# Mixer A's lowest score level: products over the feature axis instead of window matmuls

## The chip, the cores and the metric

The kernel runs on one core of a Trainium2 chip. The metric is the device time of one execution in microseconds. Engines are called TensorE (PE in the profile, with its weight loads as PEld), VectorE (DVE), ScalarE (ACT), GpSimd (POOL) and SyncE (SP).

## The reference

A two-layer trunk over 512 tokens of width 2048, all in float32. Layer A is an HGRN2 mixer, layer B a forgetting attention; each has 16 heads of 128 features. The part that matters here is layer A's recurrence:

```
proj = rmsnorm(x) @ w_in          # q, fz, i, gate
log_f, k = from fz and a lower bound
S_t = diag(exp(log_f_t)) S_{t-1} + k_t v_t^T ;  o_t = S_t^T q_t
o = head_rmsnorm(o) * silu(gate);  x = x + o @ w_out
```

Unrolled, o_t is a sum over s <= t of score(t, s) v_s, with

```
score(t, s) = sum over features f of q_t[f] * k_s[f] * exp(b_t[f] - b_s[f])
b = cumulative sum of log_f
```

The decay depends on the feature, so scores are not a plain product of q and k.

## The kernel before

Tensors lie features by tokens, 128 x 512 for a head. Each float32 matmul is made of three: both sides are split in a high part in TensorE's float32r format and a low part (`split`, L439: ScalarE copies the high part, VectorE subtracts it), and high x high, low x high and high x low are summed in PSUM.

**Projections.** `group` (L220) multiplies 16 chunks (`kt`) of a weight block of 512 columns by the normalised input, 12 matmuls of 512 columns a chunk (L238-240 for values, L242-244 for the rest). Each chunk's weights arrive by DMA as `wr` and are split into `wh` and `wl`, three buffers each, one chunk ahead of use (`Chunks`, `w_split`). In layer A sixteen groups run in the order `q0 v0 q1 q2 v1 q3 g0 q4 v2 q5 q6 v3 q7 g1 g2 g3`; a `q` group gives q and the forget logits of two heads.

**Heads.** `mix_a(h)` (L606) is a generator: it emits one head's work in steps, each ending in `yield`. After each weight chunk `pump` runs two steps (`RATE_A = 2`), head after head; other places run steps when they need a head's buffers. Thus a head's work lies among the matmuls of later groups. The Tile framework orders the instructions of every engine by a simulated time line while building; each engine then runs its own queue in that order.

**Scores by levels.** A window is 128 tokens. Scores are computed in levels: pairs (t, s) within groups of 4 tokens (the lowest level), then groups of 16 and 64 (the loop over m = 4, 16), then halves of a window, then window against window. On each level q is first multiplied by decays for a distance d of 1, 2 or 3 (tile `e` and, on higher levels, `t1`, `tn`), so that a plain product with k gives scores. `win_scores` (L585) multiplies a window's k (`kh`, `kl`) by a row of q variants (`mh`, `ml`) into a PSUM bank, and `put_scores` (L575) copies, with a 0/1 mask (`masks`, `COPY_PREDICATED`, L583), those scores that belong to distance d into the score tile `at`, of 4 windows by 128 keys by 128 queries.

The lowest level (L624-657) takes q itself (d = 0, 128 columns a window) and three products `pr` (96, 64 and 32 columns a window): 320 columns for each of four windows, three matmuls each. A product for distance d is only wanted at queries t whose position in the group of 4 is at least d, and against one key, s = t - d; the matmul computes it against all 128 keys of the window, and the mask picks the wanted one. After the splits, q and k are multiplied in place by decays for the next level (L640, L645).

**A sum over features.** `sum_parts` (L328), used for norms, sums 128 partitions exactly: VectorE adds the lower half of the partitions to the upper (L333), VectorE makes the high part (L334) and the low part (L335) into the two halves of one tile, and a matmul with a 128 x 128 matrix of ones (L336) gives every output partition the total.

**After the scores**, `attend` multiplies them by the split values, `out_norm` norms the head, and the output projection follows once all heads are done. Layer B repeats the pattern with `mix_b`.

## Time and profile before

| what | value |
|---|---|
| time, median of 3 runs | 2014.63 us (2012.73 to 2015.29) |
| profiled execution, its time | 2013.94 us |
| span of that execution, first to last instruction | 2012.2 us |
| mean granted TensorE clock | 0.994 |
| busy share of the span: PE, DVE, ACT, POOL | 98%, 77%, 56%, 9% |
| matmuls | 10218 |
| chain that ended last: PE, DVE, DMA | 84%, 7%, 4% |

Rows of instruction groups give line, engine, operation, output and inputs, shapes and count, then total busy time and the mean time of one. In a time line the first column is the start, the second how long the merged instructions lasted from the first start to the last end. On one engine the next instruction can start before the last has ended, so the distance between starts can be shorter than the duration. Layer A's groups and heads take the span from about 50 to 850 us, its output projection goes to about 1050, layer B's groups to about 1850, its output projection to the end.

### The profile page before, as it was taken

To read this page: it belongs to the slowest core of one execution; us is meant where nothing else is said; L and a number is where in the kernel's file an instruction comes from. 1 tells how busy PE (TensorE), PEld (TensorE's weight loads), DVE (VectorE), ACT (ScalarE), POOL (GpSimd) and SP (SyncE) were. 2 spreads that over 40 slices of the span, in tenths; PEclk is the share of its full clock that TensorE was granted. 3 is DMA by queue.
4 is the path that set the end of the run, shared out by engine and by line. 5 is a ranking of instruction groups with operands and counts; after the bars stand their busy time and mean duration, and the time that the engine had idled before them with its cause. 6 is when DMAs were issued, how large, how long until landed. Compare 5 with 4: busy or idle time off the path is not lost.

```text
span 2012.2 us, 28874 instructions
## 1 busy us (share of the span) xinstructions
PE 1978.6 (98%) x10218; PEld 1696.5 (84%) x10218; DVE 1558.8 (77%) x3321; ACT 1130.1 (56%) x2311; POOL 172.8 (9%) x301
## 2 busy tenths in 40 slices
PE   9999999999999999989999999999999999999898
PEld 7888888888888888869987888888888888888898
DVE  7968987979798889698873677776766676688877
ACT  5646655657566466654443555655555556576332
POOL 3303110202122030000000000000000000000000
PEclk9999999999999999999999999999999999999999
DMA  5222222222222222244433222333233232223443
GB/s 189 74 87 82 74 84 75 83 79 79 84 74 74 74 84 84 84 142 140 149 118 95 94 87 87 95 89 95 84 89 93 92 95 89 90 84 111 132 156 105
DMA packets 61696, 195.01 MB, mean 97 GB/s; under 512 B 7904, under 2 KB 8032, under 8 KB 61552
## 3 DMA queue, kind: packets, MB, share of 16 engines
q1 hardware_dynamic: 61408, 193.17, 30.8%
q8 instruction: 80, 1.31, 0.3%
q14 instruction: 64, 0.52, 0.1%
q10 hardware_dynamic: 144, 0.01, 0.0%
HBM read 184.73 MB, written 8.42 MB: 96 GB/s over the span
## 4 chain that ended last, share of the span: by engine, by line
PE 84%; DVE 7%; DMA 4%; issue 2%; ACT 1%; POOL 1%; SPq 0%; DVEq 0%; ACTq 0%; POOLq 0%
PE gm L244 17%; PE gm L242 17%; PE gm L243 17%; PE gm L238 6%; PE gm L240 6%; PE gm L239 6%; DMA wr<-in_wb_q 2%; DVE w7l L441 2%; PE mx L590 2%; PE mx L589 2%; PE mx L588 1%; DMA wr<-in_wa_q 1%; PE mx L435 1%; PE mx L436 1%; PE mx L434 1%
## 5 line engine op out<-in xcount | busy, mean ns | idle before, releaser
L242 PE MATMUL gm<-xh,wh 128*128 128x512 f32 x1664 | 650.6, 392 | 0.1
L243 PE MATMUL gm<-xl,wh 128*128 128x512 f32 x1664 | 649.8, 391 | 0.0
L244 PE MATMUL gm<-xh,wl 128*128 128x512 f32 x1664 | 610.3, 392 | 1.1 <-DVE wl L441 1.1
L242 PEld LDWEIGHTS gm<-xh,wh 128*128 128x128 f32 x1664 | 313.1, 188 | 63.1 <-ACT wh L440 0.3
L243 PEld LDWEIGHTS gm<-xl,wh 128*128 128x128 f32 x1664 | 313.2, 188 | 62.7
L244 PEld LDWEIGHTS gm<-xh,wl 128*128 128x128 f32 x1664 | 311.3, 188 | 63.6 <-DVE wl L441 2.3
L440 ACT CAST wh<-wr 128x512 fp32r<-128x512 f32 x288 | 177.3, 620 | 155.7 <-PE gm L243 113.8
L441 DVE TENSOR_TENSOR wl<-wr,wh 128x512 fp32r<-128x512 f32 x288 | 204.7, 714 | 66.8 <-ACT wh L440 56.8
L147 ACT ACTIVATE wh<-wr,v_b_norm_w 128x256 fp32r<-128x256 f32 (+1 forms) x192 | 111.7, 584 | 186.4 <-PE gm L243 152.3
L148 DVE SCALAR_TENSOR_TENSOR wl<-wr,v_b_norm_w,wh 128x256 fp32r<-128x256 f32 (+1 forms) x192 | 109.3, 571 | 133.5 <-ACT wh L147 128.3
L239 PE MATMUL gm<-wl,xh 128*128 128x512 f32 x512 | 200.7, 392 | 0.0
L240 PE MATMUL gm<-wh,xl 128*128 128x512 f32 x512 | 200.2, 392 | 0.0
L238 PE MATMUL gm<-wh,xh 128*128 128x512 f32 x512 | 180.5, 392 | 1.5 <-DVE q L552 1.5
L147 ACT ACTIVATE wh<-wr,v_kv_norm_w 128x256 fp32r<-128x256 f32 (+1 forms) x192 | 110.1, 574 | 65.2 <-PE gm L240 48.3
L148 DVE SCALAR_TENSOR_TENSOR wl<-wr,v_kv_norm_w,wh 128x256 fp32r<-128x256 f32 (+1 forms) x192 | 109.3, 571 | 42.1 <-ACT wh L147 41.5
L583 DVE COPY_PREDICATED at<-masks,mx 128x128 f32<-128x128 uint8 (+4 forms) x448 | 108.8, 297 | 13.4 <-PE mx L590 13.0
L942 POOL TENSOR_SCALAR_AFFINE_SELECT s<-s 128x128 f32<-128x128 f32 x64 | 28.5, 445 | 1029.1 <-DVE s L941 1028.6
L238 PEld LDWEIGHTS gm<-wh,xh 128*128 128x128 f32 x512 | 95.9, 188 | 20.4 <-DVE q L552 1.8
L240 PEld LDWEIGHTS gm<-wh,xl 128*128 128x128 f32 x512 | 96.2, 188 | 19.0
L239 PEld LDWEIGHTS gm<-wl,xh 128*128 128x128 f32 x512 | 96.3, 188 | 18.8
L440 ACT CAST w7h<-wr 128x768 fp32r<-128x768 f32 x48 | 40.1, 835 | 100.7 <-PE mx L296 38.2
L440 ACT CAST kh<-k 128x512 fp32r<-128x512 f32 (+1 forms) x96 | 56.3, 587 | 44.1 <-PE mx L589 19.7
(225 smaller groups left out, 3852.6 us busy)
## 6 DMA issues: line engine op xcount, KB each, us to landing
wr<-in_wb_qk SPq DMA_DIRECT2D x64, 512.0 KB, 3.5
wr<-in_wa_qf SPq DMA_DIRECT2D x62, 512.0 KB, 3.5
wr<-in_wa_v SPq DMA_DIRECT2D x32, 512.0 KB, 3.5
wr<-in_wa_g SPq DMA_DIRECT2D x32, 512.0 KB, 3.5
wr<-in_wb_v SPq DMA_DIRECT2D x32, 512.0 KB, 3.5
wr<-in_wb_g SPq DMA_DIRECT2D x32, 512.0 KB, 3.5
wr<-in_wa_q SPq DMA_DIRECT2D x24, 512.0 KB, 3.5
wr<-in_wb_q SPq DMA_DIRECT2D x24, 512.0 KB, 3.6
```

Of the source, the lines that this page charges most:

```text
L147: S.activation(h[:, c], r[:, c], AF.Copy, scale=w[:, kt : kt + 1])
L148: V.scalar_tensor_tensor(l[:, c], r[:, c], w[:, kt : kt + 1], rd(h)[:, c], op0=ALU.mult, op1=ALU.subtract)
L238: PE.matmul(banks[j], xh, h, start=f, stop=False)
L239: PE.matmul(banks[j], xh, l, start=False, stop=False)
L240: PE.matmul(banks[j], xl, h, start=False, stop=e)
L242: PE.matmul(banks[j], h[:, c], Xh[kt], start=f, stop=False)
L243: PE.matmul(banks[j], h[:, c], Xl[kt], start=False, stop=False)
L244: PE.matmul(banks[j], l[:, c], Xh[kt], start=False, stop=e)
L440: S.copy(h, src)
L441: return V.tensor_sub(l, src, rd(h))
L583: V.copy_predicated(out, mv, data)
L589: PE.matmul(lv[:, base : base + n], kh[:, c], ml, start=False, stop=False)
```

## The change

In the lowest level the products are taken by elements. VectorE multiplies q by k (`p0`, 512 columns, distance 0), and the decayed, shifted q by k shifted back by d tokens (`pr`, 384, 256 and 128 columns for d = 1, 2, 3). `half_parts` adds the two partition halves of such a tile and puts the high part (ScalarE) and the low part (VectorE) into the two halves of another; a matmul with `ones` sums over the features. Its 128 output rows are all the same row of scores, and the masks of before pick, for each key, the columns of the queries at distance d, now for all four windows in one masked copy per distance. k is no longer split on this level. The tile `p0` takes a buffer of the tag `kl`; the two halves' tiles take one pair of `mh` and `ml`, where there were two pairs. The level takes two steps fewer of the generator.

```diff
+    def half_parts(x, hl):
+        half = P // 2
+        V.tensor_add(x[:half], x[:half], x[half:])
+        S.copy(hl[:half], x[:half])
+        V.tensor_sub(hl[half:], x[:half], rd(hl)[:half])
...
-        kh, kl = k_split(h, k)
-        pr = mt("pr", (P, NW, 192), 1)
-        for d, c0 in ((1, 0), (2, 96), (3, 160)):
+        p0 = rd(mt("kl", (P, T), 2, F32R))
+        pr = mt("pr", (P, 768), 1)
+        V.tensor_mul(p0, q, k)
+        for d, c0 in ((1, 0), (3, 384), (2, 512)):
             n = 4 - d
-            V.tensor_mul(
-                view(pr, c0, [[192, NW], [n, 32], [1, n]]),
-                view(q, d, [[P, NW], [4, 32], [1, n]]),
-                view(e, (d - 1) * T + d, [[P, NW], [4, 32], [1, n]]),
-            )
+            o = view(pr, c0, [[n, P], [1, n]])
+            V.tensor_mul(o, view(q, d, [[4, P], [1, n]]), view(e, (d - 1) * T + d, [[4, P], [1, n]]))
+            V.tensor_mul(o, o, view(k, 0, [[4, P], [1, n]]))
         yield
-        for w0 in (0, 2):
-            mh, ml = m_tiles(h)
-            for dst, src, step, n in ((0, q, P, P), (P, pr, 192, 192)):
-                d = [[320, 2], [1, n]]
-                split(view(src, w0 * step, [[step, 2], [1, n]]), view(mh, dst, d), view(ml, dst, d))
-            if w0:
-                (q and k times their decays, as below)
+        hl, hl0 = m_tiles(h)
+        half_parts(p0, hl0[:, :T])
+        half_parts(pr, hl)
+        V.tensor_mul(view(q, 0, [[4, P], [1, 4]]), view(q, 0, [[4, P], [1, 4]]), view(e, 0, [[4, P], [T + 1, 4]]))
+        kv = view(k, 0, [[4, P], [1, 3]])
+        V.tensor_mul(kv, kv, view(e, 2 * T + 3, [[4, P], [-T, 3]]))
+        yield
+        for x, w, parts in (
+            (hl0, T, ((0, 0),)),
+            (hl, T, ((1, 0), (3, 384))),
+            (hl[:, T:], 256, ((2, 0),)),
+        ):
+            lv = lv_bank()
+            PE.matmul(lv[:, :w], ones, x[:, :w], start=True, stop=True)
+            for d, c0 in parts:
+                put_scores(at, lv, 0, NW, c0, (4 - d) * 32, 1, d, d)
             yield
-            for i in range(2):
-                lv = lv_bank()
-                c = slice(i * 320, (i + 1) * 320)
-                win_scores(lv, 0, w0 + i, kh, kl, mh[:, c], ml[:, c], 320)
-                for d, c0 in ((0, 0), (1, P), (2, P + 96), (3, P + 160)):
-                    put_scores(at, lv, w0 + i, 1, c0, T, 1, d, d)
-                yield
```

## The prediction

> **What bounds the kernel now.** I read the first and fourth parts of the page, then the busy time of the engines by stretches. In the stretches the columns are the stretch, its length, the busy time of PE, PEld, DVE, ACT and POOL with instruction counts, the granted clock, the DMA share and GB/s.

> ```profile
> span 2012.2 us, 28874 instructions
> PE 1978.6 (98%) x10218; PEld 1696.5 (84%) x10218; DVE 1558.8 (77%) x3321; ACT 1130.1 (56%) x2311; POOL 172.8 (9%) x301
> ...
> PE 84%; DVE 7%; DMA 4%; issue 2%; ACT 1%; POOL 1%; SPq 0%; DVEq 0%; ACTq 0%; POOLq 0%
> ```
> ```profile
> 50.00:850.00 800.00, 797.42 (x3923) 676.30 (x3922) 685.35 (x1665) 493.40 (x1089) 126.94 (x204) 1.00 0.26 80
> ...
> 1850.00:2012.00 162.00, 145.69 (x1100) 139.95 (x1099) 126.27 (x211) 58.54 (x73) 0.00 (x0) 0.97 0.40 130
> ```

> TensorE sets the end: 84% of the chain. The change lies in mixer A, whose heads run beside the input projections from 50 to 850 us. There TensorE is busy for 797.4 of 800 us, so every matmul taken away is time, as long as nothing else takes over. VectorE is the candidate: 685 of 800 us, 86%, before anything is added. An average over 800 us hides what matters, so I cut out the stretches in which VectorE is densest:

> ```profile
> 70.00:100.00 30.00, 30.00 (x152) 25.48 (x151) 29.93 (x83) 17.22 (x44) 10.54 (x20) 1.00 0.24 71
> 170.00:210.00 40.00, 40.00 (x203) 34.18 (x202) 39.62 (x97) 23.86 (x58) 15.30 (x24) 1.00 0.26 78
> 230.00:250.00 20.00, 20.00 (x104) 17.06 (x103) 19.94 (x57) 12.93 (x35) 2.58 (x6) 1.00 0.24 79
> 350.00:390.00 40.00, 39.73 (x196) 33.37 (x196) 39.57 (x99) 26.97 (x63) 15.45 (x24) 1.00 0.25 80
> 450.00:500.00 50.00, 50.00 (x250) 42.68 (x249) 48.67 (x123) 36.53 (x91) 16.01 (x25) 1.00 0.27 84
> 550.00:590.00 40.00, 38.90 (x197) 32.92 (x196) 39.38 (x104) 25.97 (x62) 12.79 (x21) 1.00 0.24 78
> 600.00:630.00 30.00, 30.00 (x155) 25.66 (x154) 29.94 (x79) 20.12 (x48) 7.76 (x13) 1.00 0.21 70
> 730.00:770.00 40.00, 39.83 (x199) 33.72 (x198) 39.83 (x104) 24.16 (x59) 12.34 (x19) 1.00 0.25 73
> ```

> Adding up the rows: in 290 us VectorE is busy for 286.9, 98.9%, and TensorE for 288.5. Both engines are full at once. The same stretches for the multiply of q by its decay alone (L640, once a head, behind this level's products) count eleven of the sixteen heads; one of the eight rows and their sum:

> ```profile
> 170.00:210.00 40.00, 2.26 (x2) 1.00 0.26 78
> ...
> sum 290.00, DVE 12.08; mean DVE 1.51
> ```

> At 1.1 us each 12.08 us are eleven. So most of the levels that the change rewrites stand where VectorE has no time to give.

> **The change part by part.**

> TensorE. Per head twelve matmuls of 320 columns go (four windows, three products each) and three with the ones come, of 512, 512 and 256 columns. What a pipelined matmul costs is the distance between starts:

> ```profile
> 602.36 0.30 PE L588 MATMUL mx<-mh,kh 128*128 128x320 f32 x1
> 602.50 0.31 PE L589 MATMUL mx<-ml,kh 128*128 128x320 f32 x1
> 602.65 0.31 PE L590 MATMUL mx<-mh,kl 128*128 128x320 f32 x1
> 602.80 0.39 PE L240 MATMUL gm<-wh,xl 128*128 128x512 f32 x1
> 603.03 0.40 PE L238 MATMUL gm<-wh,xh 128*128 128x512 f32 x1
> ```

> Three of 320 columns take 0.44 us, 0.147 each; one of 512 takes 0.23. The 256 columns I price at the row above them, 0.147. Per head 12 x 0.147 - (0.23 + 0.23 + 0.147) = 1.15 us less, for 16 heads 18.4 us. If VectorE keeps up, that is the whole result.

> VectorE, removed and added. Here too the distance between starts counts, since short instructions overlap. A stretch of this very level (the first row merges eight copies of several widths):

> ```profile
> 184.49 1.55 DVE L583 COPY_PREDICATED at<-masks,mx 128x128 f32<-128x128 uint8 x8
> 185.91 0.55 DVE L441 TENSOR_TENSOR ml<-q,mh 128x384 fp32r<-128x384 f32 x1
> 186.38 0.45 DVE L583 COPY_PREDICATED at<-masks,mx 128x64 f32<-128x64 uint8 x2
> 186.60 0.60 DVE L441 TENSOR_TENSOR ml<-pr,mh 128x384 fp32r<-128x384 f32 x1
> 187.11 0.47 DVE L583 COPY_PREDICATED at<-masks,mx 128x96 f32<-128x96 uint8 x2
> 187.40 0.70 DVE L441 TENSOR_TENSOR kl<-k,kh 128x512 fp32r<-128x512 f32 x1
> 188.00 0.56 DVE L692 TENSOR_TENSOR q<-q,t 128x384 f32<-128x384 f32 x1
> 188.47 0.45 DVE L583 COPY_PREDICATED at<-masks,mx 128x32 f32<-128x32 uint8 x2
> 188.70 0.73 DVE L441 TENSOR_TENSOR wl<-wr,wh 128x512 fp32r<-128x512 f32 x1
> ```

> Fourteen masked copies take 1.42 + 0.22 + 0.29 + 0.23 = 2.16 us, 0.154 each. A two-operand instruction of 512 elements takes 0.60 us and one of 384 0.47, so 1.02 ns an element: 0.34 for 256, 0.21 for 128.

> ```profile
> 620.08 0.88 DVE L628 TENSOR_TENSOR pr<-q,e 128x384 f32<-128x384 f32 x2
> 620.88 0.60 DVE L729 COPY at<-mx 64x128 f32<-64x128 f32 x2
> 621.40 0.38 DVE L628 TENSOR_TENSOR pr<-q,e 128x128 f32<-128x128 f32 x1
> 621.70 0.68 DVE L441 TENSOR_TENSOR wl<-wr,wh 128x512 fp32r<-128x512 f32 x1
> ```

> The three shifted products by the decay take 0.80 + 0.30 = 1.10 us; they stay. The fold of partition halves has a relative in `sum_parts`:

> ```profile
> 214.00 0.69 DVE L441 TENSOR_TENSOR vl<-v,vh 128x512 fp32r<-128x512 f32 x1
> 214.72 0.69 DVE L333 TENSOR_TENSOR t<-t 64x512 f32<-64x512 f32 x1
> 215.44 0.42 DVE L334 CAST sl<-t 64x512 fp32r<-64x512 f32 x1
> 215.90 0.68 DVE L335 TENSOR_TENSOR sl<-t,sl 64x512 fp32r<-64x512 f32 x1
> 216.61 0.69 DVE L562 SCALAR_TENSOR_TENSOR t<-z,t 128x512 f32<-128x512 f32 x1
> ```

> Half the partitions save nothing: 512 elements take 0.72 and 0.71 us from start to start, more than the 0.60 of a full tile, because they do not overlap with their neighbours.

> Removed per head: the low part of k (0.60), the low parts of q and of the products (2 x 0.34 + 2 x 0.47 = 1.62), sixteen masked copies (2.46): 4.68 us. Added: q times k (0.60); three multiplies by shifted k, priced like those by the decay (1.10); two folds and two low parts, of 512 elements (0.72 + 0.71) and of 768 (0.26 more each: 0.98 + 0.97), 3.38; four masked copies of 512, 384, 256 and 128 elements, priced like two-operand work (0.60 + 0.47 + 0.34 + 0.21 = 1.62). Together 6.70. VectorE gets 2.0 us more per head, 32 us over the stage. Ends: 1.6 if the halves overlap like the rest (0.46 less), 2.9 if the wide copies save nothing against the sixteen narrow ones (0.84 more). I take 2.0, since its rows are of the same shapes.

> [...]

> ScalarE loses the high parts of k, q and products and gets two half-tile copies; it is busy for 493 of 800 us in the stage, so its own idle time covers the copies and I cost them at nothing; without that cover they would be two copies of some 0.7 us a head. GpSimd's work and all DMAs stay. The two steps fewer per head in the generator let a head run through in nine weight chunks, not ten: the same VectorE work is asked for in less TensorE time, which goes the same way as the sum below and is left to its upper end. The new waits: the low part waits for ScalarE's copy, with the weight split of the next chunk queued behind it on VectorE; TensorE waits for that split.

> The sum. The eleven heads in the dense stretches bring VectorE to 286.9 + 11 x 2.0 = 308.9 us where TensorE would need 290 - 11 x 1.15 = 277.4. VectorE then sets the time there: 18.9 us longer than the 290 of now, less what TensorE can run ahead on weights already split. How much that is shows in the tightest place: the split at 621.70 above ends at 622.38, and TensorE first uses it (as `wl`, L239) at

> ```profile
> 622.89 0.39 PE L239 MATMUL gm<-wl,xh 128*128 128x512 f32 x1
> ```

> 0.5 us later. Three buffers allow two chunks of lead, 2 x 12 x 0.23 = 5.5 us, so the ends are 0.5 and 5.5 a stretch; these stretches are saturated and drain the lead, so I take 1 us, near the measured row, 8 us in all. The five other heads lie where VectorE is busy for 685.4 - 286.9 = 398.5 of 510 us, 78%; there TensorE's gain comes through, 5 x 1.15 = 5.8 us. 18.9 - 8 - 5.8 = +5 us on the span of 2012.2, 2017; the profiled execution took 2013.94, 1.7 more than its span, so 2019. The median of the runs, 2014.63, is 0.7 above that execution: 2020. With 1.6 us a head the sum is +1, with 2.9 +15; with no lead at all and 2.9, +23.

> **Rivals.**

> Hidden (faster): the program's order is laid out anew, and VectorE's 32 us go into the 115 us that it idles from 50 to 850. Against it: nearly all of that idle time lies outside the dense stretches. For it: 685 + 32 = 717 of 782 us is only 92%. All hidden gives 2014.6 - 18.4 = 1996; with 2.5 us of lead a stretch, 18.9 - 20 - 5.8 = -7, 2008. It decides the sign from 1.7 us of lead a stretch on.

> Copies at full duration (faster): the sixteen masked copies would be worth more than I credit, some 0.22 us each by the two-copy rows (0.45 for two), so 1.1 us a head more saved and only 0.9 added; 11 x 0.9 = 10 us, 6.9 over the 290, swallowed by the lead; 1996 to 2003. Against it: the starts above. [...]

> Worse (slower): the added work comes as one block. In two successive steps VectorE now gets 0.60 + 1.10 + 1.10 + 3.38 = 6.2 us and the two decay multiplies before the first matmul of the head, against 0.60 + 1.10 + 0.81 before. If the block stops the weight split everywhere, all 16 heads pay 3.7 us less the lead of 1 and get little back: 16 x 2.7 - 18.4 = +25, 2040.

> Clock (slower): the granted clock is 0.97 where TensorE has holes (145.7 of 162 us busy, the row from 1850). Stalls of that kind in mixer A would cost 3% of the stretches, 9 us: 2029. [...] Against it: the longest wait of TensorE for VectorE in the stage is short:

> ```profile
> PE gm L238 <- DVE q L552: 1.5, 2, 1.0
> ```

> **How the numbers follow.** No change to be told from noise is within 0.2%, 4 us. Forecast, VectorE over its limit in the dense stretches, 2016 to 2030: 0.42, of which 0.07 falls within 4 us of before. Worse or clock: 0.15. Hidden wholly or in part, copies included: 0.43, of which 0.30 is beyond 4 us and 0.13 within. So faster 0.30, same 0.20, slower 0.50. The range goes from nearly all hidden, 1997, to between the upper sum and the block, 2035; alone the forecast would span 2014 to 2030.

> **What would show it.** Right: TensorE instructions down by 144 matmuls, VectorE's busy time from 50 us to the end of the stage up by some 30 us, its dense stretches longer, and new waits of `gm` matmuls (L244, L239) for `wl` that sum to 15 to 30 us. Wrong: the stage shorter by over 10 us with no waits for `wl`; masked copies of 512 elements far from 0.6 us; folds that overlap.

## The result, and the profile after

The changed kernel takes 2056.86 us (median of 4 runs, 2056.72 to 2057.89); the kernel before, run beside it, 2013.68 us (2010.52 to 2015.29). The ratio is 1.0215 [1.0203, 1.0227]: slower by 43 us, where 5 had been forecast and the range ended at 2035. All times below are compared with runs of the kernel before on the same chip.

The first lines of the page, after:

```profile
span 2055.0 us, 28359 instructions
PE 1984.9 (97%) x10074; PEld 1690.2 (82%) x10074; DVE 1603.9 (78%) x3177; ACT 1118.9 (54%) x2263; POOL 170.2 (8%) x301
...
PE 70%; DVE 18%; DMA 6%; issue 4%; ACT 2%; SPq 0%; DVEq 0%; ACTq 0%
```

144 matmuls are gone, and yet TensorE's busy time rose from 1978.6 to 1984.9 us (at half clock a matmul of 512 columns lasts 0.63 us, at full clock 0.39: the rows from 379.96 and 386.54 us below). VectorE has 45.1 us more in 144 fewer instructions, and its share of the chain went from 7 to 18%. The stretch of 800 us in mixer A that was shown before:

```profile
50.00:850.00 800.00, 761.77 (x3583) 633.98 (x3582) 699.37 (x1466) 453.57 (x985) 124.70 (x204) 0.97 0.24 75
```

TensorE now idles 38 of 800 us (before 2.6), at a granted clock of 0.97 (before 1.00). Over the whole span the view by core says the same, first before, then after:

```profile
core 0: 2012.2 us, clock 0.994
```
```profile
core 0: 2055.0 us, clock 0.984
```

So there are two losses. The clock cost (1 - 0.994) x 2012.2 = 12.1 us before and (1 - 0.984) x 2055.0 = 32.9 after: 20.8 more. TensorE's waits make the rest: 42.8 (span) - 20.8 (clock) + 18.4 (matmuls saved, as predicted) = 40 us. Counted from the busy times instead, TensorE's time without a matmul grew from 33.6 to 70.1 us, by 36.5. What TensorE waits for from 50 to 925 us (columns: total, times, longest):

```profile
PE gm L242 <- DVE z L393: 9.9, 3, 4.6
PE mx L595 <- DVE at L590: 6.7, 5, 2.0
PE mx L442 <- DVE al L448: 6.2, 5, 2.5
PE mx L595 <- ACT mh L447: 5.9, 5, 1.8
PE mx L654 <- DVE mh L343: 2.5, 1, 2.5
PE gm L242 <- ACT v L428: 2.5, 2, 1.6
PE mx L596 <- DVE ml L448: 2.1, 4, 1.2
...
PE gm L239 <- DVE wl L448: 0.9, 1, 0.9
PE gm L244 <- DVE wl L448: 0.3, 1, 0.3
```

The waits for split weights (`wl`), on which the prediction had counted, are 1.2 us. The waits are for mixer operands, score tiles (`at`, L590), splits of scores (`al`) and, at the start of a group, for VectorE to read the bank before (`z`, L393). In the kernel before the same stretch has, besides 8.4 us at the stage's end, waits of 1.5 and 1.0 us. How such a wait becomes two losses is seen from 379 us on. VectorE's time line:

```profile
373.34 0.95 DVE L341 TENSOR_TENSOR pr<-pr 64x768 f32<-64x768 f32 x1
374.33 0.88 DVE L646 TENSOR_TENSOR k<-k,e 128x384 f32<-128x384 f32 x1
...
376.50 0.95 DVE L343 TENSOR_TENSOR mh<-pr,mh 64x768 fp32r<-64x768 f32 x1
377.49 1.28 DVE L448 TENSOR_TENSOR ml<-q,mh 128x384 fp32r<-128x384 f32 x1
378.70 1.57 DVE L448 TENSOR_TENSOR kl<-k,kh 128x512 fp32r<-128x512 f32 x1
...
381.06 0.48 DVE L679 TENSOR_TENSOR pr<-q,t 128x128 f32<-128x128 f32 x1
381.47 0.68 DVE L448 TENSOR_TENSOR wl<-wr,wh 128x512 fp32r<-128x512 f32 x1
...
383.22 0.54 DVE L448 TENSOR_TENSOR ml<-pr,mh 128x384 fp32r<-128x384 f32 x1
```

and TensorE's:

```profile
379.96 0.39 PE L244 MATMUL gm<-xh,wl 128*128 128x512 f32 x1
382.14 0.47 PE L595 MATMUL mx<-mh,kh 128*128 128x192 f32 x2 [1.79 <-ACT mh L447]
383.82 0.53 PE L596 MATMUL mx<-ml,kh 128*128 128x192 f32 x1 [1.21 <-DVE ml L448]
...
386.54 0.63 PE L243 MATMUL gm<-xl,wh 128*128 128x512 f32 x1
386.97 0.63 PE L244 MATMUL gm<-xh,wl 128*128 128x512 f32 x1
387.40 0.63 PE L242 MATMUL gm<-xh,wh 128*128 128x512 f32 x1
```

VectorE runs without a gap, and the folds and two stretched splits (1.28 and 1.57 us) make it late. TensorE's queue has the next level's matmuls (L595, L596) first, and it waits 1.79 and 1.21 us for their operands. The first of them is a copy by ScalarE (`mh`), which itself waits for VectorE's product at 381.06. After that matmuls of 512 columns start 0.43 us apart, not 0.23. The same place by stretches (length, PE busy, granted clock, DMA share, GB/s):

```profile
379.00:384.00 5.00, 2.00 (x10) 0.97 0.00 2
384.00:391.00 7.00, 7.00 (x23) 0.53 0.22 77
391.00:396.00 5.00, 5.00 (x24) 1.00 0.00 0
```

Three us of waiting are paid once more as nearly 7 us at half clock. The clock record of the trace has nine such spells in mixer A, at a clock of 0.50, between 100 and 855 us: five of 3.41 and four of 6.83 us, 44.4 us together. The kernel before has none there. At half clock they cost half of that, 22 us, close to the 20.8 of the ledger.

### The profile page after: what moved, and what is told of

Read it like the earlier page. It is cut to its first block, busy times and chain, and to the rows that moved or that the text cites. A ratio compares the mean times of both kernels' runs of the same rounds, so it can differ in the third digit from the quotient of the medians.

```text
span 2055.0 us, 28359 instructions
## 1 busy us (share of the span) xinstructions
PE 1984.9 (97%) x10074; PEld 1690.2 (82%) x10074; DVE 1603.9 (78%) x3177; ACT 1118.9 (54%) x2263; POOL 170.2 (8%) x301
## 4 chain that ended last, share of the span: by engine, by line
PE 70%; DVE 18%; DMA 6%; issue 4%; ACT 2%; SPq 0%; DVEq 0%; ACTq 0%
PE gm L242 16%; PE gm L244 16%; PE gm L243 16%; PE gm L238 4%; PE gm L239 4%; PE gm L240 4%; DMA wr<-in_wa_q 3%; DVE wl L448 2%; DMA wr<-in_wb_q 2%; DVE w7l L448 2%; DVE at L590 2%; PE mx L442 1%; PE mx L443 1%; PE mx L958 1%; PE mx L596 1%
## 5 line engine op out<-in xcount | busy, mean ns | idle before, releaser
L244 PE MATMUL gm<-xh,wl 128*128 128x512 f32 x1664 | 605.8, 394 | 1.0 <-DVE wl L448 1.0
L244 PEld LDWEIGHTS gm<-xh,wl 128*128 128x128 f32 x1664 | 313.9, 189 | 65.4 <-DVE wl L448 2.3
L239 PE MATMUL gm<-wl,xh 128*128 128x512 f32 x512 | 202.3, 395 | 0.9 <-DVE wl L448 0.9
L240 PE MATMUL gm<-wh,xl 128*128 128x512 f32 x512 | 201.0, 393 | 0.0
L238 PE MATMUL gm<-wh,xh 128*128 128x512 f32 x512 | 178.2, 395 | 1.2 <-DVE q L559 1.1
L238 PEld LDWEIGHTS gm<-wh,xh 128*128 128x128 f32 x512 | 96.6, 189 | 21.7 <-ACT wh L447 1.3
L239 PEld LDWEIGHTS gm<-wl,xh 128*128 128x128 f32 x512 | 97.2, 190 | 20.3 <-DVE wl L448 1.3
L240 PEld LDWEIGHTS gm<-wh,xl 128*128 128x128 f32 x512 | 97.1, 190 | 19.6
L590 DVE COPY_PREDICATED at<-masks,mx 128x128 f32<-128x128 uint8 (+5 forms) x256 | 96.9, 402 | 9.4 <-PE mx L597 4.2
L447 ACT CAST ah<-mx 128x384 fp32r<-128x384 f32 (+2 forms) x128 | 46.2, 371 | 50.7 <-PE mx L958 20.0
```

The costliest lines, as they stand in the source:

```text
L238: PE.matmul(banks[j], xh, h, start=f, stop=False)
L239: PE.matmul(banks[j], xh, l, start=False, stop=False)
L240: PE.matmul(banks[j], xl, h, start=False, stop=e)
L244: PE.matmul(banks[j], l[:, c], Xh[kt], start=False, stop=e)
L447: S.copy(h, src)
L590: V.copy_predicated(out, mv, data)
```

## The experiments

Theories: *overload* (VectorE's added work is the cause; TensorE's saving is worth nothing beside it) against *density* (fewer steps per head crowd the same work), *block* (the folds stand in one row ahead of a head's first matmul), *queue placement* (TensorE's order puts the waiting matmuls too early), *chains* (TensorE waits for each head's chain of work however the heads are spread) and *shape* (folds over half the partitions are what hurts).

**Steps given back.** Two empty steps behind the lowest level, 20 a head as before:

```
                 put_scores(at, lv, 0, NW, c0, (4 - d) * 32, 1, d, d)
             yield
+        yield
+        yield
```

> The changed kernel with two empty steps behind each head's lowest level, so that a head again takes 20 steps of the generator, ten weight chunks. Theory (overload): VectorE has more work in the dense stretches than fits beside TensorE's, and its amount sets the time; it is unchanged here, so 2050 to 2060 us. Rival (density): the head's work is asked for in one chunk less; giving the chunk back returns 2.7 us for each of eleven heads, 2025 to 2035. Rival (block): the row of folds ahead of the first matmul stops TensorE; the block stands, 2050 to 2060.

2041.94 us, 1.0145 [1.0128, 1.0162], between the two ranges: neither held. Mean clock 0.990 over a span of 2038.9 us, so 20.4 us lost in place of 32.9: 12.5 of the 15 us gained are clock. TensorE's idle time from 50 to 850 us is nearly the same (34.5 against 38.2). The nine spells of half clock in mixer A, 44.4 us, have become five of 3.41 us, 17.1 us.

**No folds.** Products split whole, six matmuls with the ones:

```
-        half_parts(p0, hl0[:, :T])
-        half_parts(pr, hl)
...
+        split(p0, hi0, lo0)
+        split(pr, hi, lo)
...
-            PE.matmul(lv[:, :w], ones, x[:, :w], start=True, stop=True)
+            PE.matmul(lv[:, :w], ones, x[:, :w], start=True, stop=False)
+            PE.matmul(lv[:, :w], ones, y[:, :w], start=False, stop=True)
```

> The changed kernel without the fold of partition halves: each product tile is split whole into a high and a low part, and both are multiplied with the ones, so three more matmuls a head (TensorE 0.6 us a head below before, where the change is 1.15 below) and about 2.1 us a head less on VectorE. 18 steps as in the change. Overload: VectorE is only 0.7 us a head above before, so 2000 to 2018 us, and the granted clock is back at 0.99. Density: the same 18 steps, so 2040 to 2055. Block: the block ahead of the first matmul is 4.5 us long against 6.5 in the change and 2.5 before, so halfway, 2030 to 2040.

2025.73 us, 1.0062 [1.0047, 1.0077]: 31 us better than the change, but still slower than before. It lies outside all three ranges: above overload's, below those of density and block.

```profile
PE 1979.0 (98%) x10122; PEld 1686.5 (83%) x10122; DVE 1569.4 (77%) x3145; ACT 1119.5 (55%) x2263; POOL 172.2 (9%) x301
```

VectorE still has 10.6 us more than before. Without the folds both VectorE's work and the block are smaller, so this run does not tell the two apart.

**VectorE work alone.** The kernel before, with dummy multiplies ahead of the level's products:

```
+        for n in (T, T, T, T, 384):
+            V.tensor_mul(view(pr, 0, [[1, n]]), q[:, :n], k[:, :n])
```

> The kernel before, with five multiplies more on VectorE in each head's lowest level (four of 512 and one of 384 elements, 2.9 us a head) whose results nobody reads; TensorE's work, the 20 steps and the chain from products to matmuls are as before. Overload: as slow as the change or slower, since TensorE gets no relief: 2055 to 2075 us, with the granted clock below 0.99. Density: no change of steps, 2010 to 2025. Block: the fill stands ahead of the first matmul as a block of the same length but without the waits between VectorE and ScalarE, 2025 to 2050.

2035.79 us, 1.0112 [1.0097, 1.0128]. VectorE's busy time rose by 40.4 us to 1599.2, the time by 0.0112 x 2012.45 (before, beside it) = 22.5: 0.56 us per us. Density is ruled out as the only cause. Overload had the sign, but 2055 to 2075 us were expected of it; 2036 lies in the range of the block, whose place the dummy work takes. Dummy work elsewhere in the head was not tried, so amount and block are not told apart by this run either.

**TensorE saving alone.** The kernel before, one of three products a window:

```
-                win_scores(lv, 0, w0 + i, kh, kl, mh[:, c], ml[:, c], 320)
+                PE.matmul(lv[:, :320], kh[:, (w0 + i) * P : (w0 + i + 1) * P], mh[:, c], start=True, stop=True)
```

> The kernel before, with one of the three products (high by high) left out of none but kept alone on the lowest level: eight of twelve matmuls of 320 columns a head are left out, 1.17 us a head, as much as the change saves; VectorE and ScalarE as before. Overload and its rivals alike say that TensorE's saving comes through when VectorE's work stays: 18.7 us less, 1993 to 1998. If VectorE already sets the time in the dense stretches of before, only the five heads outside gain, 2003 to 2010.

2018.92 us, 1.0032 [1.0021, 1.0043]: slower, where a gain had been expected of all theories. From 50 to 850 us:

```profile
sum 800.00, PE 781.51 PEld 655.43 DVE 680.71 ACT 489.86 POOL 126.97; mean PE 781.51 PEld 655.43 DVE 680.71 ACT 489.86 POOL 126.97
```

TensorE idles 18.5 us; what it saved, it waits:

```profile
PE gm L242 <- ACT v L421: 4.8, 3, 2.7
PE gm L242 <- DVE z L386: 3.9, 4, 1.6
PE gm L238 <- DVE q L552: 2.9, 1, 2.9
PE mx L589 <- DVE ml L441: 2.5, 2, 2.0
```

This run and the dummy multiplies, each about one side of the change taken alone (the multiplies 40.4 of its 45.1 us on VectorE), add up to 6.4 + 22.5 = 29 us. That is what the change costs with its two steps given back (0.0145 x 2012.45 = 29). The other 14 us of the change come with the two steps fewer, and half clock accounts for nearly all of them: (44.4 - 17.1) / 2 = 13.7 us.

**Heads spread wider.** `RATE_A = 1.5` instead of 2 (steps a weight chunk), on the change, on the kernel before, without folds, and with the TensorE saving alone:

> The changed kernel with RATE_A 1.5, not 2: a head's 18 steps spread over twelve weight chunks, not nine, and the pauses between the heads become shorter. VectorE's and TensorE's work is unchanged. Overload in dense stretches: the same VectorE work over more TensorE time, so the waits of 47 us and the halved clock of 18 us mostly go: 2000 to 2020 us. Rival (chains: TensorE's queue waits for each head's folds however the heads are spread): the waits stay, 2040 to 2057.

> The kernel before with RATE_A 1.5: 20 steps over 13.3 chunks. It waits only 5 us in mixer A, so overload gives 2006 to 2013 us. Rival (a slower rate brings heads late, and later steps that need their buffers force them through in one go): 2015 to 2040.

> The changed kernel without folds (whole tiles split, six matmuls with the ones) and RATE_A 1.5. TensorE is 9.8 us below before and VectorE 11 us above; its 19 us of waits at rate 2 should go when the heads are spread: overload 1998 to 2008 us, the fastest so far; chains or late heads 2020 to 2030.

> The kernel before with eight of the twelve matmuls of the lowest level left out (one of the three products kept) and RATE_A 1.5. At rate 2 TensorE's saving of 18.8 us came back whole as 20 us of waits and 4 us of halved clock. Overload: with the heads spread VectorE has the time, and the saving comes through, 1992 to 2000 us. Rival (VectorE and TensorE are bound to each other by chains, whatever the density): 2015 to 2022 as at rate 2.

2040.63 us (1.0131 [1.0116, 1.0146]), 2015.82 (1.0011 [1.0001, 1.002]), 2027.7 (1.0068 [1.0053, 1.0083]) and 1999.19 (0.9928 [0.9913, 0.9942]). The last says why the saving had been lost: 8 of 12 matmuls less are worth 14.5 us once the same VectorE work is asked for over more chunks. TensorE is then busy for 794.7 of 800 us, and the largest waits of the stage but one are 2.7 and 1.1 us:

```profile
PE mx L295 <- ACT w7h L440: 9.6, 1, 9.6
PE gm L242 <- ACT v L421: 2.7, 1, 2.7
PE mx L588 <- DVE at L583: 1.1, 1, 1.1
```

(The 9.6 us at the end of the stage were 8.4 before.) This is the only one of the four that came out as overload expected. The change at 1.5 steps lies in the range of chains (2040 to 2057), not in overload's (2000 to 2020); TensorE still idles 31.9 us from 50 to 880 us, where it idled 38.2, and its two largest waits are for splits of scores (`al`, 10.2 us) and for ScalarE's copy of `v` (8.4), not for folds. The kernel before and the one without folds lie in the ranges given to late heads or chains. The change itself gains 16 us and the kernel without folds nothing, so density is part of the change's cost, not all.

**Without GpSimd's two large sums.** GpSimd is the suspect for the stretched instructions. Without its sums the decays are no longer those of the reference:

```
-        G.tensor_add(e[:, 1, 1:], g[:, 1:], g[:, :-1])
-        G.tensor_add(e[:, 2, 2:], e[:, 1, 2:], g[:, :-2])
...
-        S.activation(e[:, 1, 1:], e[:, 1, 1:], AF.Exp)
+        S.activation(e[:, 1, 1:], g[:, 1:], AF.Exp)
```

> The changed kernel without GpSimd's two large sums of each head (ScalarE takes its exponentials of the decay from g itself; the decays are then not those of the reference). Nothing else is changed. In the change the folds' low parts take 1.17 us, not 0.98, and the multiplies by k 0.60, not 0.48, while GpSimd runs. Theory (VectorE is over its limit, whatever stretches it): it gets some 0.5 us a head back, and the heads' first products come some 2.5 us earlier: 2040 to 2050. Rival (GpSimd's own length starts the late chains): 2015 to 2035.

2028.59 us, 1.0061 [1.0044, 1.0078]; GpSimd's busy time fell from 170.2 to 127.8 us and VectorE's from 1603.9 to 1576.3, though it issues the same 3177 instructions:

```profile
PE 1973.8 (97%) x10074; PEld 1684.1 (83%) x10074; DVE 1576.3 (78%) x3177; ACT 1116.8 (55%) x2263; POOL 127.8 (6%) x269
```

So some 28 us of VectorE's busy time are instructions stretched while GpSimd works; the low part of 768 elements (L343), for one, lasts 0.96 us here and 1.14 in the change. The time lies below overload's range (2040 to 2050), which had counted on 8 us of stretch, and in the rival's (2015 to 2035), by which GpSimd's own length starts the late chains. The edit takes away both, so the two are not told apart. The kernel before makes the same sums, so they are not what the change added, but they belong to what fills the dense stretches.

**Matmuls later in TensorE's queue.** Three empty steps between preparation and matmuls, one here, the others ahead of the next level's banks, on the change and without folds:

```
         V.tensor_mul(kv, kv, view(e, 2 * T + 3, [[4, P], [-T, 3]]))
         yield
+        yield
...
```

> The changed kernel with three empty steps, one between the folds and the matmuls with the ones and one ahead of the matmuls of each of the next two levels, 21 steps in all. Theory (TensorE's own queue: a head's matmul is placed ahead of weight matmuls that are ready, and waits there for VectorE): with the head's matmuls half a chunk later in the program the waits of the mixer's matmuls, 26 of the 47 us, fall below 10, 2015 to 2030, below the 2042 of two empty steps behind the level. Rival (amount alone): only the steps count, 2035 to 2042.

> The changed kernel without folds (whole tiles split, six matmuls with the ones) and with the three empty steps of the run with the delay. Queue theory: most of its 19 us of waits go, 2006 to 2014, level with before or a little faster. Amount: 2020 to 2026, as without the empty steps.

2041.68 us (1.0126 [1.0111, 1.0141]) and 2031.97 (1.0078 [1.0063, 1.0093]). The first is the time of the two empty steps behind the level (2041.94), the second is slower than without the delay and outside both ranges. The waits of the mixer's matmuls, which were to fall below 10 us, are 20.2 us in the first, against 23.4 in the change. Queue placement falls, for a delay of half a chunk.

**VectorE work taken away in doses.** First the multiplies by shifted k are left out of the change, then the adds of halves as well:

```
-            V.tensor_mul(o, o, view(k, 0, [[4, P], [1, n]]))
```
```
-        V.tensor_add(x[:half], x[:half], x[half:])
```

> The changed kernel without the three multiplies by the shifted k (the products then lack k): 1.25 us a head less on VectorE, 20 us in all; steps, folds, matmuls and chains stay. Amount: taking 34 us off VectorE by leaving out the folds, with 8.6 us more on TensorE, gave back 31; so 20 us give back 18 to 25: 2032 to 2039. Block or chain of folds: the folds stand, 2048 to 2057.

> The changed kernel without the three multiplies by the shifted k and without the two adds of partition halves (the products then lack k and the upper features): VectorE's work falls by 2.9 us a head to that of before, TensorE keeps the saving of 18.4 us. Amount: like the kernel before with as many matmul columns less and VectorE untouched, 2008 to 2020, with 15 to 25 us of waits, and not the 1996 of TensorE's saving. Rival (the folds' own waits and the multiplies were the harm, and VectorE at the old amount is harmless): 1994 to 2003.

2032.01 us (1.0076 [1.0061, 1.0091]) and 2017.25 (1.0012 [1.0003, 1.0022]), both in overload's ranges; the block of folds, left standing in the first, had asked for 2048 to 2057. The second and the saving-alone kernel are different codes with equal work on both engines, page against page:

```profile
PE 1969.7 (98%) x10074; PEld 1677.0 (83%) x10074; DVE 1556.1 (77%) x3097; ACT 1118.1 (55%) x2263; POOL 175.8 (9%) x301
```
```profile
PE 1968.1 (98%) x10090; PEld 1680.4 (83%) x10090; DVE 1556.1 (77%) x3321; ACT 1128.4 (56%) x2311; POOL 172.2 (9%) x301
```

Their ratios, 1.0012 and 1.0032, differ by 0.2%, against 2.15% for the change. Shape falls: the low parts over half the partitions still stand in the second, and it is as fast as the kernel that has none.

**The other end.** The kernel before with only the high parts in the lowest level:

```
-        kh, kl = k_split(h, k)
+        kh, _ = k_tiles()
+        S.copy(kh, k)
...
-                split(view(src, w0 * step, [[step, 2], [1, n]]), view(mh, dst, d), view(ml, dst, d))
+                S.copy(view(mh, dst, d), view(src, w0 * step, [[step, 2], [1, n]]))
...
```

> The kernel before with only the high parts in the lowest level: four matmuls for twelve, 18.8 us less on TensorE, and no low parts of k, q and products there, about 2.2 us a head, 35 us, less on VectorE. Amount of VectorE's work decides: with the same matmuls and VectorE's work of before it took 2019; now TensorE's saving comes through, 1992 to 1999. Rival (the laid-out order decides, not the amount): 2010 to 2020.

2002.64 us, 0.994 [0.9924, 0.9957]: 4 us short of overload's range and well outside the rival's. With 33 us less on VectorE than the saving alone it is 16 us faster.

Kernels with two steps a chunk and 18 to 19 us less TensorE work, by VectorE's busy time (the kernel before, beside them, took 2012.5 to 2015.8). The last column is the time at half clock in mixer A, by the clock records of the traces:

| kernel | VectorE busy, us | clock | time, us | half clock, us |
|---|---|---|---|---|
| high parts only | 1523.0 | 0.992 | 2002.6 | 6.8 |
| saving alone | 1556.1 | 0.991 | 2018.9 | 10.2 |
| change, no multiplies, no adds | 1556.1 | 0.992 | 2017.3 | 10.2 |
| change, no GpSimd sums | 1576.3 | 0.987 | 2028.6 | 27.3 |
| change, no multiplies | 1582.6 | 0.989 | 2032.0 | 20.5 |
| change, matmuls delayed | 1602.1 | 0.990 | 2041.7 | 17.1 |
| change, two steps given back | 1602.7 | 0.990 | 2041.9 | 17.1 |
| the change | 1603.9 | 0.984 | 2056.9 | 44.4 |

The time rises by about 0.5 us per us of VectorE's work. The change lies 15 us above that line: two kernels with its load take 2042, and their 27 us less at half clock are worth 14 of the 15. So the load sets most of the cost, and the two steps fewer add to it through the clock. The edits share little but VectorE's load; that each also moves the order of the other work was not separated from it.

No exact version beat the kernel before. The two faster ones, the saving alone at 1.5 steps (1999) and high parts only (2003), leave low parts out.

## Why the prediction was wrong

*TensorE, -18.4 us:* 144 matmuls fewer, as said; and taken alone that much work less is worth nothing at this rate (1.0032). The step that the five heads outside the dense stretches let their 5.8 us through failed. What was saved came back as waits, 18.5 us of the stage in that run, although VectorE is busy for only 680.7 of 800 us; where those five heads lost theirs is not shown.

*VectorE, 2.0 us a head:* 45.1 / 16 = 2.8 us, within the ends given (1.6 to 2.9) but at the upper one. Groups by shape from 50 to 925 us:

```profile
L343 DVE TENSOR_TENSOR mh<-pr,mh 64x768 fp32r<-64x768 f32 x16 | 18.3, 1141 | 0.5
...
L590 DVE COPY_PREDICATED at<-masks,mx 128x512 f32<-128x512 uint8 x16 | 11.7, 733 | 0.9 <-PE mx L654 0.8
L590 DVE COPY_PREDICATED at<-masks,mx 128x384 f32<-128x384 uint8 x16 | 11.7, 732 | 0.6 <-PE mx L654 0.4
L590 DVE COPY_PREDICATED at<-masks,mx 128x256 f32<-128x256 uint8 x16 | 11.7, 731 | 2.9 <-PE mx L654 2.7
...
L341 DVE TENSOR_TENSOR pr<-pr 64x768 f32<-64x768 f32 x16 | 15.3, 954 | 0.5
...
L639 DVE TENSOR_TENSOR pr<-pr,k 128x384 f32<-128x384 f32 x16 | 10.7, 669 | 0.2
```

The wide copies were the mis-sized term. All last 0.73 us; from start to start (taking each instruction up to the next start or its own end) they cost on average 0.64, 0.64, 0.58 and 0.39 us for 512, 384, 256 and 128 elements, where 0.60, 0.47, 0.34 and 0.21 had been taken. All masked copies together saved 0.3 us a head, not 0.84. The rest is small: splits saved 2.0 a head, not 2.2, the folds and their low parts cost 3.5, not 3.38 (the 768-element low part lasts 1.14 us, 0.18 of it stretch by GpSimd's sums), the multiplies 1.2, not 1.10. That the folds do not overlap was right (373.34 + 0.95, next start 374.33).

*The lead, -8 us:* this step failed outright. TensorE hardly waits for `wl` (1.2 us from 50 to 925); it waits for the mixer's own operands, which stand in its queue between the projection's matmuls. Weights split ahead do not help there. Without the lead, and without the 5.8, the prediction's own sum is 286.9 + 11 x 2.8 - 290 = +28 us.

*Two steps fewer a head, put at nothing:* the prediction saw that the same work would be asked for in nine chunks, not ten, and left that to the upper end of its range. Giving the steps back returned 15 us, 12.5 to 13.7 of them clock.

*Clock:* taken as a rival of 9 us, at 0.15 together with the block of folds. It cost 20.8 us, since some stalls within the stage are followed by whole spells at half clock (nine, 44.4 us); the 0.97 that I had read at the end of the program is an average over such spells (6.83 us from 1875.43 and 3.45 us from 2008.55, of 162 us) and full clock. The longest-wait row of before, 1.0 us, was no evidence: it told of a stage without the added work. In the changed kernel two waits of 1.79 and 1.21 us, with one short pair of matmuls between them, were followed by 6.83 us at half clock; in the 3.41 us ahead of this spell TensorE was busy for 0.49 us.

28 + 21 = 49 us, where 43 were measured; with the 0.56 us per us of the dummy multiplies in place of the eleven heads, 45.1 x 0.56 + 20.8 = 46 (those multiplies had a small clock loss of their own: 0.992 in their run against 0.994 before, some 4 us). Both sums were made with the result known, and the clock's share holds that of the two steps.

*Block of folds:* its price, 2040, lay nearer, but for another reason: leaving out the multiplies alone, with the folds left standing, already gave back 25 us, and empty steps, behind the block or behind its matmuls, give 15 us. A part of the block is not ruled out: one wait of 2.5 us is for a fold's low part (L654 for L343), and the dummy multiplies stood in the same place.

*Open:* why two steps or a delay leave TensorE's waits nearly as long (34.5 us from 50 to 850 us) but let fewer of them fall so that half clock follows; why the delay and the lower rate do not help, or hurt, without folds; and why VectorE's work is worth about half its time, which fits idle time outside the dense stretches but was not tested by itself.

## What to carry to other kernels

When two engines are both nearly always busy in the same stretches (here 98.9% and 99.5% of 290 us), price a trade between them by the engine that gets more, and give the other's saving no value until its own removal has been tried alone. Price a change in how densely the work is asked for as a term of its own. Look whose operands stand next in the waiting engine's queue before crediting any lead. Add the clock to every new stall in TensorE: here it made half of the loss (20.8 of 43 us).

## What the runs showed of the hardware that was not expected

Masked copies from PSUM into four strided windows last 0.73 us for 128, 256, 384 and 512 elements alike, against 0.26 to 0.30 for copies of 32 to 128 elements into one window (groups of before by shape, 50 to 925 us):

```profile
L583 DVE COPY_PREDICATED at<-masks,mx 128x64 f32<-128x64 uint8 x128 | 32.0, 259 | 0.1
...
L583 DVE COPY_PREDICATED at<-masks,mx 128x96 f32<-128x96 uint8 x64 | 18.5, 301 | 0.2
```

Not every wait costs clock. Stretches of after (length, PE busy, granted clock, DMA share, GB/s):

```profile
78.00:82.00 4.00, 2.96 (x14) 1.00 0.05 8
...
104.00:107.00 3.00, 0.78 (x4) 1.00 0.39 158
107.00:111.00 4.00, 3.70 (x12) 0.57 0.46 133
```

A wait of 1.04 us left the clock at 1.00; one of 2.52 us was followed by 0.57, an average over 3.41 us at half clock and the rest at full.

GpSimd's two sums, 42 us of its busy time, stretch VectorE's instructions by some 28 us (its busy time was 1576.3 us without them, 1603.9 with them): a split of 512 elements, 0.68 us at 381.47, took 1.57 at 378.70, where the second sum runs from 378.44 to 379.72. Not all of GpSimd's work does this: the split at 381.47 ran beside one of its short additions (381.48 to 382.42).
